# Two more expert outputs kept on the chip at the end of the second mixture of experts

## The chip, the core and the metric

The program runs on one core of a Trainium2 chip. The core has five engines with lists of instructions of their own: TensorE (PE in the profile, its weight loads as PEld), VectorE (DVE), ScalarE (ACT), GpSimd (POOL) and SyncE (SP, which here only issues transfers). Sixteen DMA engines move data between the chip's memory and the core's on-chip memory. The metric is the time of one execution on the device, in microseconds (us).

## The reference

Two transformer blocks run one after the other on 512 tokens of width 1024. Only the end of the second one is touched: a hierarchical mixture of experts. Every token picks one of four groups and two of the eight experts in it, so each of the 32 experts gets few tokens. What is computed there is

```python
combine = jnp.sum(one_hot(expert_idx, 32) * weights[..., None], axis=1)
y = zeros_like(hf)
for e in range(32):
    he = silu(hf @ w_gate[e]) * (hf @ w_up[e])
    y = y + combine[:, e:e+1] * (he @ w_down[e])
return x + y
```

with `w_gate[e]` and `w_up[e]` of 1024 x 256 and `w_down[e]` of 256 x 1024.

## The kernel before

Each expert of block 2 works on at most 64 slots (T = 64). `moe_experts_rows` (L1127) goes over the experts in 16 pairs. For each expert, `gather` brings its tokens into `xe` by products with a one-hot matrix, `gu` (L1172) multiplies by four gate/up weight tiles of 512 KB (line L1179) and applies SiLU, `htr` transposes the pair's result into `hT`, and `down` (L1198) multiplies by two down-weight tiles of 512 KB (L1208). `down` of a pair runs while `gu` of the next pair runs. The two halves of the 1024 output columns lie in the two halves of the 128 partitions, so an expert's output is one 128 x 512 tile.

What happens to that output differs by expert. `LAST` is the number of last experts whose outputs stay on the chip.

- Experts 0 to E - LAST - 1 (0 to 29 before): ACT or DVE scales the output into one of three buffers `yy` (L1218 for odd experts, L1220 for even ones), and POOL issues an indirect transfer that adds the rows to the accumulator `xa` in the chip's memory (L1221). This is called a scatter below. All scatters write `xa`, and each waits for the one before to land.
- Behind the scatter of expert E - LAST - 1, SP issues four loads of 512 KB that bring `xa` back into four buffers (`spare<-xa`, L1227). They are called base loads below. They wait for the last scatter.
- The last LAST experts (30 and 31 before): the output is split into a high part (ACT, L1213) and a low part (DVE, L1214) in a `spare` buffer.

`tokens` (L1135) makes one-hot matrices for these last experts on DVE (L1143), four tiles of 128 x 128 for each. At the end, for each of four token tiles and both column halves, `combined` multiplies the one-hot matrix with the high and the low parts (L1271), DVE adds the base tile (L1253), and the result is stored (L1255, L1261). Products for the two column halves use different 64 rows of PE and run side by side.

The weights are streamed by SP into 32 buffers of 512 KB (`more`, L801, issue on L823). A load waits until its buffer's reader is done and until the load four before it has landed. `spare` hands out weight buffers that are no longer needed. In `more`, two of them are set aside near the end of the stream for the one-hot matrices.

The order of instructions in each engine's list is fixed when the program is built: a scheduler with a simulated timeline merges the lists. SP takes its list strictly in order.

Of the kernel before, what the change touches and what calls it, by code (L numbers as in the profile page):

```python
# [12 lines left out]
F32R = mybir.dt.float32r  # L13
# [8 lines left out]
S = 512  # L22
# [32 lines left out]
class Kern:  # L55
# [745 lines left out]
    def more(self):  # L801


        n = len(self.places)
        while len(self.place) < len(self.seq):
            i = len(self.place)
            if i < n:
                pool, tag = self.places[i]
            else:
                while self.rows is None and self.place[self.prev][0] is None:  # L810
                    self.prev += 1
                if self.used <= self.prev:
                    return
                pool, tag = self.place[self.prev]
                self.prev += 1
                if pool is self.mw and len(self.free) < self.LAST and len(self.seq) - i <= 14:
                    self.free.append((pool, tag))
                    continue
            self.place.append((pool, tag))
            e, c = self.seq[i]  # L820
            raw = tag if pool is None else pool.tile([P, 1024], F32, tag=tag, name="raw", bufs=1)
            self.raws[e, c] = raw
            ld = self.nc.sync.dma_start(raw, self.wd[e, c - 4] if c > 3 else self.wgu[e, c])  # L823
            self.loads.append(ld.ins)
            under = self.FLIGHT if i >= n else self.FIRST
            if i >= under:
                self.tc.add_manual_dep(ld.ins, self.loads[i - under].name,
                                       mybir.DependencyInfo(mybir.DependencyClass.Sync, mybir.DependencyReason.DATA), reason="few under way")
# [298 lines left out]
    def moe_experts_rows(self, me):  # L1127
# [6 lines left out]

        def tokens():  # L1135

            st = [self.spare(F32R)[:, :S] for _ in range(LAST)]
            sh = me.tile([2 * T, LAST, NT], F32, name="sh")
            for t in range(NT):
                V.tensor_scalar(sh[:, :, t], self.sl[:, 0, E - LAST:], -128.0 * t, None, op0=OP.add)  # L1140
            for e in range(LAST):
                for t in range(NT):
                    V.tensor_scalar(st[e][:, t * P:(t + 1) * P], self.c("iota"), sh[:, e, t:t + 1], None, op0=OP.is_equal)  # L1143
            return st
# [88 lines left out]
        for p in range(E // 2 + 1):  # L1233
            e = 2 * p
            if e == E - 4:
                st = tokens()
            if e % 4 == 0:
                select(e + 4)
            for i in range(2):
                if e < E:  # L1240
                    gu(e + i)
                down(e + i - 2)
            if e < E:
                for q in range(2):
                    gather(e - e % 4 + 4, e % 4 + q)
                htr(p)
# [566 lines left out]
    def run(self, stage=99):  # L1813
# [59 lines left out]
            return  # L1873
        self.NG, self.NNAT, self.NPR, self.NATW = 6, 4, 7, 512
        nmw, nme = 19, 1
        self.LAST = 2
        self.NX, self.NY, self.FLIGHT = 0, 3, 4
        self.FIRST = 3
        xs, xl, short = [], [], ExitStack()
# [229 lines left out]
```

## Time and profile before

| | us |
|---|---|
| median of 3 runs | 1411.08 (1409.53 to 1414.77) |
| the profiled execution, its own time | 1408.74 |
| its span, first to last instruction | 1407.0 |
| PE busy | 1303.7 (93%) |
| DVE busy | 774.0 (55%) |
| ACT busy | 591.6 (42%) |
| POOL busy | 452.1 (32%) |

Times inside the execution are counted from the span's start. A timeline row gives start, length, engine, line, operation, output and inputs, the count, and in brackets how long the engine had been idle and what ended that.

### The profile page before, as it was taken

The numbers are of one execution on the slowest core, as the hardware profiler recorded it, in microseconds if no ns is written. First come the engines' busy times: TensorE is split into PE (matmuls) and PEld (weight loads), VectorE is DVE, ScalarE is ACT, GpSimd is POOL, SyncE is SP. The second block draws the span as 40 slices with busy tenths as digits, with TensorE's granted clock in tenths as the row PEclk, the third lists the DMA queues.
The fourth block names the chain that finished last, engine by engine and source line by source line (L and its number), as shares of the span: only waits on it lengthen the run. The fifth ranks groups of instructions, "written<-read, shape, count | busy, mean of one in ns | idle before, by whom it ended". The sixth has DMA issues, their size and how long they took to land.

```text
span 1407.0 us, 21509 instructions
## 1 busy us (share of the span) xinstructions
PE 1303.7 (93%) x8172; PEld 998.5 (71%) x8188; DVE 774.0 (55%) x1659; ACT 591.6 (42%) x1235; POOL 452.1 (32%) x368
## 2 busy tenths in 40 slices
PE   8898999869999798999999999999999799999983
PEld 8876777746665597987899999887789644545421
DVE  6899964858785856665455354224553723322222
ACT  5466442336664346654654354444223212221110
POOL 3354642422220336531143243123632302111211
PEclk9999999879999999999999999999999899999987
DMA  6122114889997211201121222226328589999994
GB/s 238 60 76 75 46 39 170 304 295 305 313 302 283 98 46 63 109 34 61 50 79 69 76 70 75 100 76 230 114 96 326 184 299 381 356 366 363 377 373 154
DMA packets 69124, 250.77 MB, mean 178 GB/s; under 512 B 12370, under 2 KB 12626, under 8 KB 62864
## 3 DMA queue, kind: packets, MB, share of 16 engines
q1 hardware_dynamic: 56304, 220.64, 43.2%
q0 software_dynamic: 11408, 25.24, 6.6%
q10 hardware_dynamic: 1296, 3.38, 0.6%
q8 instruction: 68, 1.11, 0.3%
q14 instruction: 48, 0.39, 0.1%
HBM read 230.29 MB, written 26.71 MB: 183 GB/s over the span
## 4 chain that ended last, share of the span: by engine, by line
PE 76%; DVE 13%; DMA 5%; ACT 2%; issue 2%; POOL 1%; SPq 0%; DVEq 0%; ACTq 0%; POOLq 0%
PE mm L181 13%; PE mm L183 13%; PE mm L182 13%; PE mm L1179 8%; PE tp L266 5%; PE pv L1164 5%; PE sc L1208 3%; DMA xa<-yy,idx 2%; PE pv L1759 2%; PE mm L1051 2%; DVE work L409 1%; DVE m L408 1%; PE sc L1733 1%; PE sc L1489 1%; DVE pr L707 1%
## 5 line engine op out<-in xcount | busy, mean ns | idle before, releaser
L154 POOL TENSOR_TENSOR wlo<-raw,whi 128x1024 fp32r<-128x1024 f32 (+4 forms) x62 | 149.6, 2416 | 252.5 <-ACT whi L153 231.9
L153 ACT ACTIVATE whi<-raw 128x1024 fp32r<-128x1024 f32 (+4 forms) x172 | 178.3, 1039 | 99.3 <-PE mm L183 42.4
L154 DVE TENSOR_TENSOR wlo<-raw,whi 128x1024 fp32r<-128x1024 f32 (+3 forms) x110 | 142.6, 1297 | 103.8 <-ACT whi L153 103.3
L1221 POOL DMA_INDIRECT xa<-yy,idx x30 | 46.4, 1548 | 220.3 <-DMA xa<-yy,idx 136.5
L183 PE MATMUL mm<-whi,hRl 128*128 128x256 f32 x384 | 108.8, 284 | 0.0
L181 PE MATMUL mm<-whi,hhi 128*128 128x256 f32 (+2 forms) x352 | 102.8, 292 | 4.8 <-ACT qraw L1428 1.8
L181 PE MATMUL mm<-whi,hRh 128*128 128x256 f32 x352 | 102.6, 292 | 0.0
L183 PE MATMUL mm<-whi,hlo 128*128 128x256 f32 (+2 forms) x352 | 101.5, 288 | 0.0
L182 PE MATMUL mm<-wlo,hhi 128*128 128x256 f32 (+2 forms) x352 | 101.0, 287 | 0.0
L1179 PE MATMUL mm<-raw,xe 128*64 128x512 f32 x396 | 100.6, 610 | 0.0
L182 PE MATMUL mm<-wlo,hRh 128*128 128x256 f32 x352 | 99.8, 283 | 0.0
L271 POOL TENSOR_TENSOR hss<-hss,mh 128x4 f32<-128x4 f32 (+1 forms) x64 | 60.1, 940 | 100.2 <-DVE hss L270 89.8
L181 PEld LDWEIGHTS mm<-whi,hhi 128*128 128x128 f32 x352 | 68.5, 195 | 10.5 <-issue 3.8
L183 PEld LDWEIGHTS mm<-whi,hRl 128*128 128x128 f32 x384 | 73.2, 191 | 0.0
L1186 DVE TENSOR_TENSOR gul<-gul,mm 64x512 f32<-64x512 f32 x32 | 21.9, 686 | 92.4 <-ACT gul L1185 92.4
L182 PEld LDWEIGHTS mm<-wlo,hhi 128*128 128x128 f32 x352 | 68.6, 195 | 1.6 <-issue 1.4
L183 PEld LDWEIGHTS mm<-whi,hlo 128*128 128x128 f32 x352 | 68.3, 194 | 1.4 <-issue 1.1
L1164 PEld LDWEIGHTS pv<-sel,xh 128*128 128x128 f32 x256 | 49.8, 194 | 27.2 <-issue 20.6
L1164 PE MATMUL pv<-sel,xh 128*128 128x256 f32 x256 | 67.1, 297 | 1.8 <-issue 1.8
L181 PEld LDWEIGHTS mm<-whi,hRh 128*128 128x128 f32 x352 | 67.2, 191 | 0.2
L182 PEld LDWEIGHTS mm<-wlo,hRh 128*128 128x128 f32 x352 | 67.2, 191 | 0.0
L1164 PE MATMUL pv<-sel,xl 128*128 128x256 f32 x256 | 65.6, 292 | 0.0
(537 smaller groups left out, 3634.4 us busy)
## 6 DMA issues: line engine op xcount, KB each, us to landing
raw<-in_wgu SPq DMA_DIRECT2D x163, 512.0 KB
raw<-in_wd SPq DMA_DIRECT2D x77, 512.0 KB
raw<-in_w2b SPq DMA_DIRECT2D x26, 1024.0 KB
rawp<-in_wgu SPq DMA_DIRECT2D x29, 512.0 KB
raw<-in_wo SPq DMA_DIRECT2D x12, 1024.0 KB
rawp<-in_wd SPq DMA_DIRECT2D x19, 512.0 KB
raw<-in_w1b SPq DMA_DIRECT2D x8, 1024.0 KB
spare<-xa SPq DMA_DIRECT2D x8, 512.0 KB
```

What stands on the lines that cost most here:

```text
L153: self.nc.scalar.activation(hi[:, :n], src, AF.Copy)
L154: eng.tensor_tensor(lo[:, :n], src, hi[:, :n].bitcast(F32), op=OP.subtract)
L181: nc.tensor.matmul(ps, lh, rh, start=start and i == 0, stop=False)
L182: nc.tensor.matmul(ps, lh, rl, start=False, stop=False)
L183: nc.tensor.matmul(ps, ll, rh, start=False, stop=stop and i == n - 1)
L266: self.nc.tensor.transpose(out, in_, self.c("ident")[:n, :n])
L271: return self.nc.gpsimd.tensor_tensor(out, out, self.mh[:, :n], op=OP.pow)
L1051: nc.tensor.matmul(pg[:T, :], x[2][:, j, :], wf[:, j * 512:(j + 1) * 512], start=False, stop=(j == 1))
L1164: nc.tensor.matmul(pg[:, j * 256:(j + 1) * 256], part[t][:, c], sels[e][:, t].rearrange("p e s -> p (e s)"), start=(i == 0), stop=(i == le ...
L1179: nc.tensor.matmul(pg[j * T:(j + 1) * T], x[:, 2 * c + j, e % 4], w[:, j * 512:(j + 1) * 512], start=(c == 0), stop=(c == 3))
L1208: nc.tensor.matmul(py[n * T:(n + 1) * T], hT[:, k, :], w[:, n * 512:(n + 1) * 512], start=(k == 0), stop=(k == 1))
L1221: nc.gpsimd.indirect_dma_start(out=xa2, out_offset=bass.IndirectOffsetOnAxis(ap=self.idx[:, 0, e:e + 1], axis=0), in_=y, in_offset=None, b ...
```

## The change

`LAST` of block 2 goes from 2 to 4. Experts 28 to 31 are kept on the chip, and 28 and 29 are scattered no more. The base loads belong to expert 27's `down` now. The one-hot matrices of two experts share one buffer of 128 x 1024, so four experts still need two buffers, and the count of buffers set aside in `more` stays two.

```diff
@@ more @@
-                if pool is self.mw and len(self.free) < self.LAST and len(self.seq) - i <= 14:
+                if pool is self.mw and len(self.free) < (self.LAST if self.rows is None else self.LAST // 2) and len(self.seq) - i <= 14:
@@ moe_experts_rows, tokens @@
-            st = [self.spare(F32R)[:, :S] for _ in range(LAST)]
+            st = [self.spare(F32R) for _ in range(LAST // 2)]
+            st = [st[i // 2][:, i % 2 * S:(i % 2 + 1) * S] for i in range(LAST)]
@@ run, block 2 @@
-        self.LAST = 2
+        self.LAST = 4
```

The diff does not show what the scheduler makes of it. On SP, at the end of the weight stream, the list before was as follows. `in_wd2` are down weights, `in_wgu2` gate/up weights, `xa_68` is the accumulator, and DMASW are the lanes of POOL's scatters.

```order
L823 DMA rawp_12009<-in_wd2 128x1024 [waits DMAHW4_49,PE_49]
L823 DMA rawp_12007<-in_wgu2 128x1024 [waits DMAHW5_49]
L823 DMA rawp_12010<-in_wd2 128x1024 [waits DMAHW6_49,PE_49]
L823 DMA rawp_12008<-in_wgu2 128x1024 [waits DMAHW7_49]
L823 DMA rawp_12013<-in_wd2 128x1024 [waits DMAHW0_49,PE_49]
L823 DMA rawp_12011<-in_wd2 128x1024 [waits DMAHW1_49,PE_49]
L823 DMA raw_13642<-in_wd2 128x1024 [waits DMAHW2_49,PE_49]
L823 DMA rawp_12012<-in_wd2 128x1024 [waits DMAHW3_49]
L1227 DMA spare_13808<-xa_68 128x1024 [waits DMASW2_49,DMASW1_49]
L1227 DMA spare_13810<-xa_68 128x1024
L1227 DMA spare_13812<-xa_68 128x1024 [waits DMASW3_49,PE_49]
L1227 DMA spare_13814<-xa_68 128x1024 [waits DMASW4_49,PE_49]
```

The same place on SP in the changed kernel:

```order
L823 DMA rawp_12009<-in_wd2 128x1024 [waits DMAHW4_49,PE_49]
L823 DMA rawp_12007<-in_wgu2 128x1024 [waits DMAHW5_49]
L1228 DMA spare_13764<-xa_68 128x1024 [waits DMASW1_49,DMASW0_49,PE_49]
L1228 DMA spare_13766<-xa_68 128x1024 [waits DMASW2_49,PE_49]
L1228 DMA spare_13768<-xa_68 128x1024 [waits DMASW3_49,PE_49]
L823 DMA rawp_12010<-in_wd2 128x1024 [waits DMAHW6_49]
L1228 DMA spare_13770<-xa_68 128x1024 [waits DMASW4_49,PE_49]
L823 DMA rawp_12008<-in_wgu2 128x1024 [waits DMAHW7_49]
L823 DMA rawp_12013<-in_wd2 128x1024 [waits DMAHW0_49]
L823 DMA rawp_12011<-in_wd2 128x1024 [waits DMAHW1_49]
L823 DMA raw_13642<-in_wd2 128x1024 [waits DMAHW5_49,DMAHW2_49]
L823 DMA rawp_12012<-in_wd2 128x1024 [waits DMAHW7_49,DMAHW3_49]
```

The four base loads have moved from behind the last weight load to a place six weight loads earlier (three base loads, one weight load, the fourth base load, then five weight loads). Everything ahead of them in SP's list is as before. `rawp_12010` holds down weights of expert 29, `rawp_12008` the last gate/up weights of expert 31, and the other four the down weights of 30 and 31.

On PE, around the second half of expert 29's `down` (`sc` from `rawp_12010`) and the last part of expert 31's `gu` (`mm` from `rawp_12008`), the list before:

```order
L1179 MATMUL mm_13785<-rawp_12007,xe_13487 64x512 [waits DMAHW1_49]
L1179 MATMUL mm_13785<-rawp_12007,xe_13487 64x512
L1208 MATMUL sc_13798<-rawp_12010,hT_13759 64x512 [waits DMAHW2_49]
L1208 MATMUL sc_13798<-rawp_12010,hT_13759 64x512
L1179 MATMUL mm_13785<-rawp_12008,xe_13487 64x512 [waits DMAHW3_49]
L1179 MATMUL mm_13785<-rawp_12008,xe_13487 64x512
L266 MATMUL tp_13816<-cf_58,gul_13770 128x128 [waits DVE_49]
L266 MATMUL tp_13816<-cf_58,gul_13770 128x128
L1208 MATMUL sc_13821<-rawp_12011,hT_13819 64x512 [waits DMAHW5_49,DVE_49]
L1208 MATMUL sc_13821<-rawp_12011,hT_13819 64x512
```

The same place in the changed kernel, with the first one-hot products, which read expert 28's output `spare_13796`:

```order
L1180 MATMUL mm_13799<-rawp_12007,xe_13487 64x512 [waits DMAHW1_49]
L1180 MATMUL mm_13799<-rawp_12007,xe_13487 64x512
L1272 MATMUL pv_13851<-spare_13796,spare_13694 128x512 [waits Activation_49]
L1272 MATMUL mm_13862<-spare_13796,spare_13694 128x512 [waits DVE_49]
L1272 MATMUL pv_13893<-spare_13796,spare_13694 128x512
L1272 MATMUL pv_13851<-spare_13796,spare_13694 128x512 [waits DVE_49]
L1272 MATMUL mm_13862<-spare_13796,spare_13694 128x512
L1272 MATMUL pv_13893<-spare_13796,spare_13694 128x512
L1209 MATMUL sc_13812<-rawp_12010,hT_13775 64x512 [waits DMAHW5_49]
L1209 MATMUL sc_13812<-rawp_12010,hT_13775 64x512
L1272 MATMUL pv_13851<-spare_13817,spare_13694 128x512 [waits Activation_49]
L1272 MATMUL mm_13862<-spare_13817,spare_13694 128x512
```

There are 64 one-hot products instead of 32. Part of those for experts 28 and 29 stand between the last weight products; 44 of the 64 stand after the last product that reads a weight, where all 32 stood before.

## Rows read from the trace of the kernel before

**Rows 1.** The page: shares of the chain that ended last; DMA busy tenths in 40 slices.

```profile
PE 76%; DVE 13%; DMA 5%; ACT 2%; issue 2%; POOL 1%; SPq 0%; DVEq 0%; ACTq 0%; POOLq 0%
...
DMA  6122114889997211201121222226328589999994
```

**Rows 2.** The chain of waits from 1352 us on: start, us, what.

```profile
1360.91 7.49 DMA xa<-yy,idx
...
1369.14 5.85 DMA xa<-yy,idx
...
1375.73 3.69 DMA xa<-yy,idx
...
1380.30 3.86 DMA xa<-yy,idx
...
1384.90 3.75 DMA xa<-yy,idx
...
1390.34 7.94 DMA spare<-xa
```

**Rows 3.** Waits of SP's queue, 1330 to 1400 us: total us, times, longest.

```profile
SPq L1227 <- DMA xa<-yy,idx: 18.8, 1, 18.8
```

**Rows 4.** Timeline of SP's issues, 1355 to 1400 us.

```profile
1360.77 0.33 SPq L823 DMA_DIRECT2D rawp<-in_wgu  x1
...
1363.33 0.33 SPq L823 DMA_DIRECT2D rawp<-in_wgu  x1
...
1369.57 0.33 SPq L823 DMA_DIRECT2D rawp<-in_wd  x1
1388.71 2.01 SPq L1227 DMA_DIRECT2D spare<-xa  x4
```

**Rows 5.** Windows: us, busy by engine, PEclk, DMA share, GB/s.

```profile
1364.00:1368.00 4.00, 4.00 (x10) 1.13 (x12) 0.42 (x1) 0.00 (x0) 0.00 (x0) 0.50 1.00 335
...
1378.00:1382.00 4.00, 3.40 (x10) 1.21 (x12) 0.45 (x2) 0.00 (x0) 1.54 (x1) 0.57 0.10 16
...
1397.00:1402.00 5.00, 0.00 (x0) 0.00 (x0) 2.57 (x4) 0.00 (x0) 0.00 (x0) 0.50 0.92 365
1402.00:1407.00 5.00, 0.00 (x0) 0.00 (x0) 0.00 (x0) 0.00 (x0) 0.00 (x0) 0.50 0.07 27
```

**Rows 6.** Timeline of DVE: one-hot matrices, low parts, final adds.

```profile
1343.51 0.89 DVE L1143 TENSOR_SCALAR spare<-cf,sh 128x128 fp32r<-128x128 f32 x4 [0.97 <-PE mm L1179]
1345.84 0.69 DVE L1186 TENSOR_TENSOR gul<-gul,mm 64x512 f32<-64x512 f32 x1 [1.45 <-ACT gul L1185]
...
1383.98 1.61 DVE L1214 SCALAR_TENSOR_TENSOR spare<-sc,gs,spare 128x512 fp32r<-128x512 f32 x2 [5.00 <-ACT spare L1213]
1392.05 0.69 DVE L1253 TENSOR_TENSOR spare<-spare,sc 128x512 f32<-128x512 f32 x1 [6.46 <-DMA spare<-xa]
...
1397.05 0.69 DVE L1253 TENSOR_TENSOR spare<-spare,sc 128x512 f32<-128x512 f32 x1 [1.79 <-issue]
...
1398.97 0.68 DVE L1253 TENSOR_TENSOR spare<-spare,tp 128x512 f32<-128x512 f32 x1
```

**Rows 7.** Timeline of PE, 1371 to 1389 us.

```profile
1374.65 1.02 PE L1179 MATMUL mm<-rawp,xe 128*64 128x512 f32 x4
...
1379.03 3.31 PE L1208 MATMUL sc<-rawp,hT 128*64 128x512 f32 x8 [0.52 <-DVE hT L1196]
1382.18 1.02 PE L1208 MATMUL sc<-raw,hT 128*64 128x512 f32 x4
1383.04 1.02 PE L1208 MATMUL sc<-rawp,hT 128*64 128x512 f32 x4
1384.88 0.48 PE L1271 MATMUL sc<-spare 64*128 64x512 f32 x1 [0.81 <-ACT spare L1213]
...
1388.50 0.39 PE L1271 MATMUL mm<-spare 64*128 64x512 f32 x1
```

**Rows 8.** Timeline of ACT: the last scaled output for a scatter.

```profile
1375.10 0.69 ACT L1218 ACTIVATE yy<-sc,gs 128x512 f32<-128x512 f32 x1 [4.48 <-DMA xa<-yy,idx]
```

## The prediction

> **What bounds the kernel now.** I read the page's chain shares and DMA slices first. PE carries 76% of the chain over the whole span, but the DMA slices are at 8 to 9 tenths through the end [rows 1], so the end needs a look of its own. The chain of waits shows it: from 1360.91 us on, no PE work stands in it at all. There is one scatter after another, each issued when the one before has landed, then a base load, then DVE's adds [rows 2]. The five rows shown are the scatters of experts 25 to 29. SP's queue says the same from its side: the first base load stood 18.8 us at the head of SP's list, waiting for the scatters [rows 3]. The last weight load had been issued at 1369.57, the base loads at 1388.71 [rows 4]. PE was done with weights at 1384.06 and with the one-hot products at 1388.89 [rows 7], and DVE still waited until 1392.05 for base data [rows 6]. So the last 9 us before 1388.7 belong to two scatters and nothing else, and after 1388.7 the end is base loads, adds and stores.
>
> **What is removed.** Scatters 28 and 29 leave the chain. Expert 27's scatter landed at 1375.73 + 3.69 = 1379.42, expert 29's at 1384.90 + 3.75 = 1388.65: 9.2 us. ACT's wait for a free `yy` buffer before expert 29 (4.48 us) goes too [rows 8], but it gains nothing: PE finished the products that ACT takes next at 1375.67 [rows 7], when that ACT row was running.
>
> **What is moved, and why it takes the gain back.** SP's list now has three base loads, a weight load, the fourth base load and five weight loads where it had six weight loads and then four base loads. SP takes its list in order, and the 18.8 us show that it stands still while the first base load waits. So six weight loads of experts 29 to 31, which were issued from 1362.1 to 1369.57, now wait for scatter 27. The weights were early before; now they are the last thing to come.
>
> Step one, when does scatter 27 land? The stream stops after the load issued at 1360.77. Four loads are then under way; at 1.28 us each (two steps from 1360.77 to 1363.33 took 2.56 [rows 4]) they drain by 1365.9. Scatter 25 is issued at 1360.91 with 5.0 us of loads beside it. Scatter 26 had 4.8 us of loads beside it (the last load, issued at 1369.57, was one of four and drained by about 1374) and took 5.85, where 25 had taken 7.49 under the full stream; scatters alone take 3.7 to 3.9 [rows 2]. The DMA share was 1.00 in the one stretch and 0.10 in the other [rows 5]. I give scatter 25 5.9 us, scatters 26 and 27 3.75 each, and 0.73 us between a landing and the next issue (1360.91 + 7.49 to 1369.14): 1360.91 + 5.9 + 0.73 + 3.75 + 0.73 + 3.75 = 1375.8, and the first base load goes at 1375.9. The ends are 1373.7 (all three at 3.75) and 1379.5 (nothing gets faster). The Trainium skill, "DMA: Bandwidth & Descriptors", section "Queues, rings and completion order", says that each DMA engine takes turns between the queues that have work, packet by packet; by it a scatter is slowed only while loads stand beside it, which gives the 1375.9, and the kernel before agrees with its 3.69 against 7.49. A scatter bound by its own fixed steps would give 1379.5.
>
> Step two, the ten loads. The first base load of before was used 1392.05 - 1388.71 = 3.34 us after its issue. Nine more at 1.28 put the last down weights at 1375.9 + 3.34 + 11.5 = 1390.8. (Before, four base loads took until 1398.28, but stores ran beside them.) The last gate/up load is the sixth and lands at 1385.6. From the end of those products to the first `down` product took 1379.03 - 1375.67 = 3.36 us before [rows 7]. With 0.9 us for its own products that is 1389.9, so it hides under the last load, by less than 1 us.
>
> Step three, from the last weights to the last add. Three pairs of `down` products of 0.43 us (the row of four took 0.86 to the next [rows 7]) end at 1392.1. High and low parts took from 1384.06 to 1385.59 before [rows 6], so the last low part is ready at 1393.6. Of the 64 one-hot products 44 stand behind the last weight product. The 32 of before took 4.0 us, 0.125 each, with the two column halves side by side [rows 7]. The first token tile's sum now has six products of one half in a row and twelve others ahead of it. I take 2.2 us from the last low part to the first add (1.0 would be PE's own last products; 4.4 the same at half the clock): 1395.8. Four adds took 1397.05 to 1399.65, 2.6 us [rows 6]; eight take 5.2. Last add: 1401.0, against 1399.65 before.
>
> Step four, the tail. From the last add to the span's end was 1407.0 - 1399.65 = 7.35 us. Now all 2 MB of stores leave within 4 us instead of 6; at the 365 GB/s of the stretch 1397 to 1402 [rows 5] they need 5.7 us and end some 0.6 us later than the last store alone would. Span: 1401.0 + 7.35 + 0.6 = 1409.0, that is 2.0 us more than 1407.0.
>
> **Edits at no cost.** Sixteen one-hot tiles instead of eight: eight more DVE instructions of 0.22 us (four in 0.89), in two groups. In the second group 0.9 us more fits in the 1.45 us that DVE was idle before its next row [rows 6]; the first stands in a similar gap. If the cover were gone it would be 1.8 us. Two more high/low pairs replace two scalings on ACT and DVE and stand before the late weights. The number of buffers set aside is the same, so the weight stream up to the base loads is unchanged.
>
> **Rivals.** One, the path simply gets 9.2 us shorter: if the end still hung on base loads alone, they would start at 1379.5 instead of 1388.7 and the time would be 1411.1 - 9.2 = 1402. The chain and the 18.8 us speak for it; the six weight loads behind the wait speak against it. It needs their 3 MB to arrive with nothing waiting on them, and PE's list waits on each.
>
> Two, on the other side: PE falls to the lower clock and stays there. In 1364 to 1368 the granted clock was 0.50 (1.2 GHz), after a pause of PE, and in 1378 to 1382 it was 0.57, after another [rows 5]; eight products took 3.15 us there and four 0.86 just after [rows 7], about twice as long each. The new gap, while SP waits (about 1374 to 1383), is longer than those, and after it PE works in short pieces between single loads. If the clock were still at half from the last weights to the last sum, the `down` products would cost 1.3 us more and the 44 one-hot products, at about 0.125, some 5.5 us more, nearly all ahead of the last add: 1409.0 + 6.5 = 1415.5 of span, 1419.6 as a median. The point that decides is whether the clock is back at 1.0 by about 1391. Before, PE got work again at 1379.03 and was at full speed at 1382.18 [rows 7]. The Trainium skill, "TensorE: Matmul & The Clock Gate", section "HAM oscillation — how this bites in real kernels", describes this case: waits for data between groups of products put PE back to half the clock each time. The trace agrees with it in both gaps; whether it lasts is not shown.
>
> Three, scatters 25 to 27 are no faster without the stream: the base loads go at 1379.5, and the time is 3.6 us over the forecast, 1416.7.
>
> **How the numbers follow.** The profiled execution took 1408.74 us, 1.74 more than its span and 2.3 below the median; the change of +2.0 is put on the median: 1413.1. The likeliest case alone spans 1409 to 1417. Chances: this forecast 0.72, rival one 0.06, rival two 0.14, rival three 0.08. Measurement tells about 0.5%, 7 us, from no change: below 1404.0 is faster, above 1418.1 slower. Rival one is the faster chance, 0.06. Slower is rival two with a little of the others' upper ends, 0.16. The rest is 0.78. The range 1407 to 1420 leaves out rival one and what lies past rival two.
>
> **What would show it.** In the changed kernel's profile: SP's longest wait is again the base load on the scatters, but ends near 1376; DMA is nearly idle from about 1366 until then; expert 31's gate/up weights land near 1386 and the last down weights near 1391, and PE waits for them; the last scatter takes about 3.7 us; the last add ends near 1401. The prediction is wrong if the base loads do not hold the weights up (last weights before 1385), if the clock stays at 0.50 past 1391, or if the ten loads take clearly more than 15 us.

## The result and the profile after

The changed kernel took 1419.1 us (median of 8 runs, 1416.4 to 1423.6), the kernel before 1408.6 us on the same chip (8 runs, 1405.1 to 1414.8). The ratio is 1.0075, 95% interval 1.0055 to 1.0094: slower by 10.6 us, and by more than the 0.5% that the prediction counted as no change. The profiled execution took 1418.33 us, with a span of 1416.6 against 1407.0 before.

The page first: the shares of the chain are those of [rows 1] almost to the digit, so the page alone tells nothing. The chain of waits (start, us, what), which answers to [rows 2], shows what came in:

```profile
1358.66 6.89 DMA xa<-yy,idx
...
1366.29 3.73 DMA xa<-yy,idx
...
1370.76 3.68 DMA xa<-yy,idx
...
1375.82 6.83 DMA rawp<-in_wd
1382.70 2.00 PE sc L1209 x4
...
1394.69 5.34 PE sc L1209 x16
```

The two last scatters of [rows 2] are gone, and the last one left, expert 27's, ends at 1374.44. But where a base load and adds followed before, PE now stands in the chain from 1382.70 on. This execution issued expert 25's scatter at 1358.66, 2.25 us earlier than the profiled one of before. SP's waits and its timeline, beside [rows 3, 4]:

```profile
SPq L1228 <- DMA xa<-yy,idx: 14.7, 1, 14.7
```

```profile
1359.41 0.33 SPq L823 DMA_DIRECT2D rawp<-in_wgu  x1
1374.49 1.28 SPq L1228 DMA_DIRECT2D spare<-xa  x3
1375.82 0.42 SPq L823 DMA_DIRECT2D rawp<-in_wd  x1
1376.34 0.40 SPq L1228 DMA_DIRECT2D spare<-xa  x1
1376.79 0.44 SPq L823 DMA_DIRECT2D rawp<-in_wgu  x1
1377.28 0.92 SPq L823 DMA_DIRECT2D rawp<-in_wd  x2
1382.72 0.33 SPq L823 DMA_DIRECT2D raw<-in_wd  x1
1385.27 0.33 SPq L823 DMA_DIRECT2D rawp<-in_wd  x1
```

No weight is asked for between 1359.41 and 1375.82. Six weight loads, which left by 1369.57 before, leave behind the first base loads. Of these, expert 31's last gate/up weights, issued at 1376.79, took 8.4 us to land, at 1385.2 (the last number of this line of the DMA issues):

```profile
rawp<-in_wgu SPq DMA_DIRECT2D x1, 512.0 KB, 8.4
```

The last load took 5.0 us and landed at 1390.3. PE's timeline and windows (us, busy by engine, PEclk, DMA share, GB/s), beside [rows 7, 5]:

```profile
1382.70 1.98 PE L1209 MATMUL sc<-rawp,hT 128*64 128x512 f32 x4 [10.81 <-DMA rawp<-in_wd]
...
1386.61 1.98 PE L1180 MATMUL mm<-rawp,xe 128*64 128x512 f32 x4
...
1394.62 4.55 PE L1209 MATMUL sc<-rawp,hT 128*64 128x512 f32 x12
1399.00 1.02 PE L1209 MATMUL sc<-raw,hT 128*64 128x512 f32 x4
```

```profile
1366.00:1368.00 2.00, 2.00 (x12) 0.58 (x10) 1.10 (x2) 0.68 (x2) 1.56 (x1) 1.00 0.00 0
...
1390.00:1394.00 4.00, 4.00 (x9) 2.59 (x10) 0.85 (x2) 0.39 (x1) 0.00 (x0) 0.50 0.00 0
1394.00:1398.00 4.00, 4.00 (x10) 1.00 (x10) 0.00 (x0) 0.00 (x0) 0.00 (x0) 0.50 0.00 0
1398.00:1402.00 4.00, 4.00 (x25) 2.34 (x23) 1.50 (x2) 1.38 (x2) 0.00 (x0) 0.98 0.00 0
```

PE waited 10.81 us. The granted clock fell during this wait (0.54 in 1374 to 1378) and was 0.50 (1.2 GHz) until 1398. In 1390 to 1398 next to no data was under way (DMA share 0.00) and PE was busy without a break: its own half speed was then the limit. Four records of `down` products took 1.98 us at 1382.70 and 1.02 at 1399.00. DVE, beside [rows 6]:

```profile
1343.37 1.66 DVE L1144 TENSOR_SCALAR spare<-cf,sh 128x128 fp32r<-128x128 f32 x8 [0.97 <-PE mm L1180]
1345.70 0.69 DVE L1187 TENSOR_TENSOR gul<-gul,mm 64x512 f32<-64x512 f32 x1 [0.68 <-ACT gul L1186]
...
1400.80 0.75 DVE L1215 SCALAR_TENSOR_TENSOR spare<-sc,gs,spare 128x512 fp32r<-128x512 f32 x1 [0.98 <-ACT spare L1214]
1403.84 0.69 DVE L1254 TENSOR_TENSOR spare<-spare,sc 128x512 f32<-128x512 f32 x1 [2.29 <-PE tp L1272]
...
1408.04 0.68 DVE L1254 TENSOR_TENSOR spare<-spare,tp 128x512 f32<-128x512 f32 x1
```

The first add starts at 1403.84 where 1395.8 was forecast, and the last ends at 1408.72 where 1401.0 was forecast.

### The profile page after: what moved, and what is told of

The parts are those of the page before. It is cut to its first block, busy times and chain, and to the rows that moved or that the text cites. A ratio compares the mean times of both kernels' runs of the same rounds, so it can differ in the third digit from the quotient of the medians.

```text
span 1416.6 us, 21589 instructions
## 1 busy us (share of the span) xinstructions
PE 1313.3 (93%) x8220; PEld 1001.5 (71%) x8220; DVE 776.1 (55%) x1668; ACT 591.9 (42%) x1236; POOL 449.3 (32%) x366
## 3 DMA queue, kind: packets, MB, share of 16 engines
q8 instruction: 68, 1.11, 0.3%
## 4 chain that ended last, share of the span: by engine, by line
PE 76%; DVE 13%; DMA 5%; issue 3%; ACT 2%; POOL 1%; SPq 0%; POOLq 0%; ACTq 0%; DVEq 0%
PE mm L181 13%; PE mm L183 13%; PE mm L182 13%; PE mm L1180 7%; PE tp L266 5%; PE pv L1165 5%; PE sc L1209 4%; DMA xa<-yy,idx 3%; PE pv L1760 2%; PE mm L1051 2%; DVE work L409 2%; DVE m L408 1%; PE sc L1734 1%; PE sc L1490 1%; DVE pr L707 1%
```

## The experiments

My theory after the result: the six weight loads held up behind the base loads cost the whole difference, partly by coming late and partly by what the gap does to PE's clock. The rivals: something else in the change is dear (shared rows, more one-hot products), or the two scatters were never worth 9 us. Ratios are to the kernel before, run on the same chip (medians 1407.8 to 1409.7 us).

Each edit makes the scheduler merge the lists anew, so the order of PE's last products differs somewhat between these kernels. From the first of the last eight `down` products on, that costs nothing: from its start to the first add it was 7.44 to 7.50 us in all seven traces that have the clock at 1.00 there, in two different orders (9.22 in the changed kernel, at half the clock for half of it). Ahead of expert 31's last gate/up product it does cost, as is told where it matters.

**Base loads on SP, behind the six weight loads.** On SP this undoes the move alone. In PE's list, the three one-hot products that stand between expert 29's second `down` half and expert 31's last gate/up product go behind the latter.

```
+ with ExitStack() as behind:
+     for ld in self.loads[-6:]:
+         behind.enter_context(self.tc.issue_after(ld))
      self.order = [nc.sync.dma_start(self.base[t], ...)]
```

> The changed kernel with one edit: the four base loads stay on SP but are kept behind the last six weight loads in its list. Theory: same as with the base loads on POOL, span 1400 to 1403, ratio 0.995 to 0.997, because only the place in SP's list matters and not which queue carries the loads. If the other queue matters (two queues share the DMA engines differently), this one differs from the POOL kernel by more than 2 us. Rival A (one-hot products cost what the scatters gave): ratio 1.000 or above.

Measured: 1401.1 us (6 runs), ratio 0.9942 (0.9920 to 0.9964). Its SP timeline, PE timeline, windows and first add:

```profile
1382.82 1.75 SPq L1231 DMA_DIRECT2D spare<-xa  x4
```

```profile
1376.06 1.08 PE L1209 MATMUL sc<-rawp,hT 128*64 128x512 f32 x4
1376.97 1.03 PE L1180 MATMUL mm<-rawp,xe 128*64 128x512 f32 x4
```

```profile
1382.00:1386.00 4.00, 4.00 (x19) 1.54 (x20) 0.39 (x1) 0.69 (x1) 0.00 (x0) 1.00 0.55 193
1386.00:1390.00 4.00, 4.00 (x27) 2.96 (x28) 1.57 (x3) 0.69 (x1) 0.00 (x0) 1.00 0.89 323
```

```profile
1389.54 0.69 DVE L1257 TENSOR_TENSOR spare<-spare,sc 128x512 f32<-128x512 f32 x1 [1.05 <-PE sc L1275]
```

The base loads leave only when scatter 27 has landed, as in the changed kernel, but nothing stands behind them: the last weight load went at 1373.07. From 1374 to 1390 PE is busy for 15.9 of 16 us at a clock of 1.00, and the first add waits for PE, not for a base load. So two scatters fewer are worth 8.2 us (0.0058 of 1407.8), and holding up six weight loads turns that into a loss of 10.6: it costs 18.8 us, give or take 4. At most 1.4 us of it can be the three one-hot products that stand elsewhere: in the changed kernel the gate/up product began that much after its weights had landed (1386.61 against 1385.2). This version beats both kernels.

**Base loads issued by POOL.** Another way to clear SP's list.

```
- self.order = [nc.sync.dma_start(self.base[t], ...)]
+ self.order = [nc.gpsimd.dma_start(self.base[t], ...)]
```

> The changed kernel with one edit: the four base loads are issued by POOL, behind the scatters in its own list, and not by SP. SP's list then holds weight loads alone. Theory (the loss is SP standing still with six weight loads behind the base loads, and the clock that falls in the pause): the weights land by about 1375 us again, the base loads start near 1379.5 and land by about 1388, the first add starts near 1388, and the span is 1400 to 1403, 4 to 7 us under the kernel before (ratio 0.995 to 0.997). Rival A (the 32 extra one-hot products and splits cost what two scatters gave): 1407 or more, ratio 1.000 or above. Rival B (the scatters and base loads themselves got slower): span near 1416, ratio near 1.0075.

Measured: 1408.1 us, ratio 0.9994 (0.9976 to 1.0011). The weights are on time, the last of them issued at 1373.49, and yet 7 us are missing against the run above. Its PE timeline, windows and first add:

```profile
1375.66 1.08 PE L1209 MATMUL sc<-rawp,hT 128*64 128x512 f32 x4
...
1378.97 1.08 PE L1180 MATMUL mm<-rawp,xe 128*64 128x512 f32 x4
1381.47 1.45 PE L1272 MATMUL mm<-spare 64*128 64x512 f32 x4 [1.41 <-DVE gul L1187]
...
1385.46 3.68 PE L1209 MATMUL sc<-rawp,hT 128*64 128x512 f32 x8
```

```profile
1382.00:1386.00 4.00, 4.00 (x11) 1.92 (x11) 0.74 (x2) 0.00 (x0) 1.95 (x4) 0.53 0.74 255
1386.00:1390.00 4.00, 4.00 (x12) 1.14 (x8) 0.00 (x0) 0.00 (x0) 0.00 (x0) 0.62 0.72 271
```

```profile
1395.46 0.69 DVE L1254 TENSOR_TENSOR spare<-spare,sc 128x512 f32<-128x512 f32 x1 [1.79 <-PE sc L1272]
```

From expert 29's second `down` half to the first add it is 19.8 us here and 13.5 in the run above: 6.3 of the 7 us lie there. PE's list differs: expert 31's last gate/up product stands behind six one-hot products more, for which PE waited 0.79 us. It starts 3.3 us after that `down` half instead of 0.9, which is 2.4 us. The other 3.9 come behind it: PE was idle for 1.41 us, and the clock then fell to half for some 7 us. By the two windows the half clock took at most 3.4 us of PE's time (an estimate: 4 us times 0.47 and 4 us times 0.38). Three theories: the order of PE's list, the half clock, or POOL as the issuer.

**POOL as the issuer in the kernel before**, the same edit there:

> The kernel before with its four base loads issued by POOL instead of SP. There the base loads stand behind all weight loads anyway, so nothing can be held up by them. If POOL's queue costs about the same as SP's: ratio 1.000 within 0.003, last add within 1.5 us of the 1399.65 of before. If issuing base loads from POOL is itself dear (the rival for why the run with base loads on POOL came out some 6 us above the one that keeps them on SP behind the weights): ratio 1.003 to 1.006.

Measured: ratio 0.9997 (0.9981 to 1.0013). Issuing from POOL costs nothing there that the interval would show.

**POOL and eight products more**, result unused, right behind expert 31's last gate/up product:

```
+ if e == 31:
+     with self.tc.issue_after(mm.ins):
+         warm = bank("pv")
+         for i in range(8):
+             nc.tensor.matmul(warm, st[0][:, :P], self.last[0][1][0], ...)
```

> The changed kernel with base loads issued by POOL, and with 8 extra one-hot products, result unused, right behind expert 31's last gate/up product, where TensorE stood idle for 0.8 and 1.4 us in the run without them and fell to half clock from 1382 to 1390. If that half clock is what separates base loads on POOL (1408.1) from base loads on SP behind the weights (1401.1): clock at 1.0 throughout 1378 to 1392, ratio 0.993 to 0.997. If POOL's queue or the later base loads are what costs: clock at 1.0 and ratio 0.998 to 1.001. If the clock falls again, nothing is told apart: ratio about 1.000.

Measured: 1405.3 us, ratio 0.9965 (0.9947 to 0.9983). By the medians, eight products of useless work made it faster by 0.3%, though the two intervals overlap a little. The windows, expert 29's second `down` half and the first add:

```profile
1374.00:1378.00 4.00, 4.00 (x14) 2.71 (x15) 1.11 (x2) 0.77 (x2) 1.03 (x3) 0.60 0.40 115
1378.00:1382.00 4.00, 4.00 (x20) 2.11 (x19) 0.42 (x1) 0.00 (x0) 1.49 (x3) 1.00 0.93 284
```

```profile
1369.55 1.08 PE L1214 MATMUL sc<-rawp,hT 128*64 128x512 f32 x4
```

```profile
1388.24 0.69 DVE L1259 TENSOR_TENSOR spare<-spare,sc 128x512 f32<-128x512 f32 x1 [2.27 <-PE sc L1277]
```

The clock dipped earlier, while the eight products ran (3.68 us), and was back before the last `down` products. From expert 29's second `down` half to the first add it is 18.7 us, 1.1 less than without the eight products. The ratios differ by 0.0029, 4 us, with an interval of some 0.6 to 7.6, which holds the 1.1. So the half clock is a part of the 7 us, but how it shares them with the order of PE's list is not shown.

**Only the shared rows**: the changed kernel with two experts kept instead of four.

```
- self.LAST = 4
+ self.LAST = 2
```

> The changed kernel with two last experts kept on the chip instead of four (so all thirty scatters of before); what is left of the change is that one-hot rows share room. SP's list is that of before. If that part is free, as the prediction has it: ratio 0.998 to 1.002. If it carries part of the loss: 1.003 or more.

Measured: ratio 1.0002 (0.9987 to 1.0017). That part is free, as the prediction had it. The 32 one-hot products more are not in this kernel; they are in the first experiment's, which beats the kernel before.

**Base loads that wait for no scatter**, still ahead of the six weight loads. They read another buffer of the same size, so the scattered sums are left out of the output.

```
- ... self.xa[t * P:(t + 1) * P, :]
+ ... self.xr[t * P:(t + 1) * P, :]   # issued behind the loads of two earlier chunks
```

> The changed kernel with the base loads in their early place on SP (now all four ahead of the six weight loads), but reading another array of the same size that was written long before, so that they wait for no scatter. The scattered sums are left out of the output. Theory (the wait costs, not the 2 MB in front of the weights): base loads go out near 1361 us, the last weights land near 1380 instead of 1390, PE has no long pause, and the span is 1400 to 1405, ratio 0.995 to 0.999. Rival (four more transfers ahead of the weights cost by themselves as much as the wait): the last weights land near 1385 or later and the span is over 1408, ratio 1.001 or above.

Measured: 1405.4 us, ratio 0.9987 (0.9969 to 1.0006), span 1403.1. Without the wait the loss is gone: it is the waiting base load at the head of the list that costs (all weight loads were issued by 1377.04 here). It is not as fast as with base loads behind the weights; its clock was 0.68 in 1378 to 1382.

**Filling the gap.** To price the half clock apart from the late weights, 48 useless one-hot products were put in front of the product that waits (expert 29's second `down` half).

```
+ if e == 29 and k == 1:
+     warm = bank("pv")
+     for i in range(48):
+         nc.tensor.matmul(warm, st[0][:, :P], self.last[0][1][0], ...)
```

> The changed kernel with 48 extra one-hot products on PE (128 rows, 512 columns, result not used) placed in its list just ahead of the product that waits for the held-up weights, so that PE is busy during the pause. SP's list is the changed kernel's, word for word. Theory (of the changed kernel's 9.6 us loss about 7 are the half clock, which lasted to about 1398 us, and 2 the late weights): the clock stays at 1.0 through the pause, the last weights land near 1390 as in the changed kernel, the last add ends near 1401 instead of 1408.7, and the span is 1408 to 1411, ratio 1.001 to 1.003. If the clock falls again in the short waits after 1383, 1411 to 1414. Rival (the clock is only a sign of waiting, the weights are the whole loss): 1416 to 1418, ratio 1.0065 to 1.008.

Measured: 1414.0 us, ratio 1.0042 (1.0025 to 1.0059). The clock stayed at 1.00 until 1386 and then fell to 0.62 in 1386 to 1390, beside two waits for weights of 1.50 and 1.08 us. So a second attempt had 64 products, in front of expert 31's last gate/up product:

```
+ if e == 31 and c == 3:
+     behind.enter_context(self.tc.issue_after(mm.ins))
+     warm = bank("pv")
+     for i in range(64):
+         wm = nc.tensor.matmul(warm, st[0][:, :P], self.last[0][1][0], ...)
+     behind.enter_context(self.tc.issue_after(wm.ins))
```

> The changed kernel with 64 extra one-hot products, result unused, in front of expert 31's last gate/up product, where TensorE otherwise waits from 1371 to 1386 us: about 14.9 us of work at 0.233 us each, ending as the gate/up weights land. Transfers and SP's list are those of the changed kernel. Theory (late weights cost about 2 us, the half clock after the gap the other 7 to 8): the granted clock stays 1.0 until the last sum, first add 1395.5 to 1398, span 1408.5 to 1411.5, ratio 1.000 to 1.003. Rival one (the late weights themselves cost most of it): clock at 1.0 and span still 1414 or more, ratio 1.004 to 1.008. Rival two (the clock falls all the same in the short waits that are left): 1411 to 1414, and the windows show 0.6 or less somewhere in 1386 to 1394.

Measured: 1417.0 us, ratio 1.0046 (1.0030 to 1.0062). PE, one window, SP and the first add; this execution's scatters were some 7 us behind the changed kernel's already at 1300 us, so only differences count:

```profile
1377.60 14.80 PE L1184 MATMUL pv<-spare 128*128 128x512 f32 x64
1393.51 1.08 PE L1187 MATMUL mm<-rawp,xe 128*64 128x512 f32 x4 [1.11 <-DMA rawp<-in_wgu]
...
1399.17 2.79 PE L1216 MATMUL sc<-rawp,hT 128*64 128x512 f32 x12
```

```profile
1390.00:1394.00 4.00, 2.89 (x15) 1.87 (x15) 0.00 (x0) 0.00 (x0) 0.00 (x0) 1.00 1.03 420
```

```profile
1381.67 1.28 SPq L1235 DMA_DIRECT2D spare<-xa  x3
```

```profile
1406.62 0.69 DVE L1261 TENSOR_TENSOR spare<-spare,sc 128x512 f32<-128x512 f32 x1 [2.27 <-PE sc L1279]
```

The clock was 1.00 in every window from 1374 to 1406, and rival one's ratio came: 1.0046, not the 1.000 to 1.003 of my theory. From the first base load to the first add it is 24.95 us here, 29.35 in the changed kernel and 19.9 in the forecast. So the half clock is worth 4.4 us there, and 4.1 by the ratios (0.0029 of 1409, with an interval of some 0.6 to 7.6). The other 6.5 us of the loss are in the late weights themselves, and that is after the 8.2 us which the scatters are worth: of the 18.8 us some 4 are the half clock and the rest, 14 to 15, the late weights.

**Three of four base loads behind the weights.** The first still waits at the head.

```
- for ld in self.loads[-6:]:
+ for ld in self.loads[-6:] if t else ():
```

(against the first experiment's edit.)

> The changed kernel with the first base load still at the head of SP's list, so that all six weight loads still wait for scatter 27, but the other three base loads behind the six weight loads. TensorE's list and scatters are little changed. It takes away 3.8 us (three loads of 1.28 us) from the time to the last weights, and leaves the wait itself and the gap. Theory (loads land one after another in the order of the list, so what stands ahead of the weights is paid in full): expert 31's gate/up weights land 5.5 to 7 us after the first base load is issued instead of 10.7, the last weights about 11 instead of 15.8, and the first add comes 4 to 5 us earlier; ratio 1.001 to 1.004 (the half clock remains). Rival (the three base loads shared the queues and cost little, and the price is the wait and the clock): ratio 1.005 to 1.008.

Measured: 1412.0 us, ratio 1.0021 (1.0000 to 1.0042). The landing of the gate/up weights, SP, PE, one window and the first add:

```profile
rawp<-in_wgu SPq DMA_DIRECT2D x1, 512.0 KB, 5.7
```

```profile
1376.61 0.33 SPq L1231 DMA_DIRECT2D spare<-xa  x1
```

```profile
1381.13 1.98 PE L1209 MATMUL sc<-rawp,hT 128*64 128x512 f32 x4 [6.17 <-DMA rawp<-in_wd]
1383.22 1.97 PE L1180 MATMUL mm<-rawp,xe 128*64 128x512 f32 x4
```

```profile
1386.00:1390.00 4.00, 3.80 (x16) 1.87 (x16) 1.40 (x3) 0.41 (x1) 0.00 (x0) 1.00 1.01 408
```

```profile
1396.72 0.69 DVE L1257 TENSOR_TENSOR spare<-spare,sc 128x512 f32<-128x512 f32 x1 [1.05 <-PE sc L1275]
```

The gate/up weights, issued at 1377.46, land 6.6 us after the first base load instead of 10.7. These 4.1 us answer to three loads of 1.28 (3.8): the loads are served in the list's order, and what stands ahead of the weights is paid for. The gate/up product starts when they land, 6.6 us after the base load instead of 12.1; the 1.4 us on top are PE's, which in the changed kernel still had three one-hot products at half the clock ahead of it and waited 0.79 us for them. The first add comes 20.1 us after that base load instead of 29.35, 9.2 us earlier and not 4 to 5. The 3.7 us that are left lie between the gate/up product and the first add (13.5 us instead of 17.2), where the clock was back from 1386 on. By the ratios the gain is 7.6 us, give or take 4.

**The same with 36 useless products in the gap.**

```
- for i in range(64):
+ for i in range(36):
```

> The same with 36 extra one-hot products, result unused, in front of expert 31's last gate/up product: 8.4 us of work where TensorE would wait from 1371 to about 1380 us. Theory: clock at 1.0 to the end; what is left is the wait for scatter 27 alone; ratio 0.997 to 1.000, about 4 us (0.3%) under the run without the products. If the clock falls all the same, or the half clock has no price once the gap is shorter: within 0.15% of that run. If the time is still 1.003 or more with the clock at 1.0, the price lies in the chain of products behind the weights, not in the order of the loads.

Measured: 1411.7 us, ratio 1.0009 (0.9994 to 1.0024), not told apart from the run before it. PE still waited 2.69 us for the gate/up weights, and the clock was 0.65 in 1386 to 1390. It did not isolate the wait for scatter 27.

## Why the prediction was wrong, and where it was right

The forecast was a change of +2.0 us; it was +10.6. The range held the time only because its upper end had been set by rival two, and rival two, at 0.14, happened: the clock was not back by 1391 but only at 1398, which the prediction had named as a sign of being wrong. The outcome "slower" had been given 0.16.

- **Step one held.** Scatters 25 to 27 took 6.89, 3.73 and 3.68 us (forecast 5.9, 3.75, 3.75), and the first base load left at 1374.49 (1375.9). The moment is partly luck: from scatter 25's issue to the base load it was 15.8 us where 15.0 was forecast, and the execution was 2.25 us early at scatter 25. The DMA share of 0.00 in 1366 to 1368 stands beside the 3.73. That is what the Trainium skill's turns between queues ("DMA: Bandwidth & Descriptors", section "Queues, rings and completion order") would give; rival three, scatters as slow as before, is out.
- **Step two held for the loads**: the last weights landed at 1390.3 (1390.8), 15.8 us after the first base load where 14.9 was forecast. Expert 31's gate/up weights landed 10.7 us after it, where 9.7 was forecast; in the runs with 48 and 64 products, where PE waited for these weights, their products began 11.3 and 11.8 us after it. I have no cause for these 1 to 2 us.
- **The end of step two and step three failed**, in two ways. Step two ended with "With 0.9 us for its own products that is 1389.9, so it hides under the last load, by less than 1 us". It did not hide. From the start of the gate/up products to the first of the last `down` products it was 8.0 us (1386.61 to 1394.62) where 4.3 was forecast; with the base loads behind the weights, at full clock, it was 5.1. The chain from the gate/up weights over activation, transposes and `down` products is the path, and the first of the last `down` products began at 1394.62, waiting for no load. Step three let three pairs of products at 0.43 us, 1.3 us, follow the last load. What follows is eight products (sixteen records) in one piece, behind eleven one-hot products and two transposes: 3.65 us at full clock (1393.19 to 1396.84 in the run with 48 products), and 5.34 here. And the clock, which step three took as full from 1391 on, was at half until 1398.
- **The ledger from the first base load to the first add**: forecast 19.9, measured 29.35. To the start of the gate/up products 12.1 instead of 9.7 (+2.4: 1.0 until the weights landed, 1.4 until PE came to them). From there to the first add 10.2 forecast, 12.6 at full clock with the base loads behind the weights, 13.1 in the run with 64 products at full clock (+2.4 to +2.9; in the latter expert 29's products come later), 17.2 in the changed kernel (+4.1 to +4.7, the clock). The span grew by 9.6 us, 7.6 more than forecast: the 9.45 of this ledger and 0.8 from step one, less the 2.25 us by which this execution was early at scatter 25 and 0.4 us in the adds and the tail.
- **Rival two was right by its sign and its deciding point; its 1419.6 is partly luck.** Over the kernel before, it put 6.5 us on the clock and 2.0 on the weights; the runs put about 4 on the clock and 6.5 on the weights. The rule of the Trainium skill that it was named beside ("TensorE: Matmul & The Clock Gate", section "HAM oscillation — how this bites in real kernels") agrees with this trace: after PE's wait for data the clock was at half, and with the wait filled it was 1.00 throughout. That it would last to 1398 with PE busy from 1390 on was what the trace of before could not show, and I gave it too little: PE waited 10.81 us, where the waits beside the two falls in the kernel before were 4.89 and 2.40, and PE's work after it came in short pieces. PE's timeline before:

```profile
1363.27 0.69 PE L266 MATMUL tp<-cf,gul 128*128 128x128 f32 x2 [4.89 <-DVE gul L1188]
...
1378.08 0.44 PE L266 MATMUL tp<-cf,gul 128*128 128x128 f32 x2 [2.40 <-DVE gul L1188]
```

- **Rival one was wrong for this kernel.** Its 1402 is what the version with base loads behind the weights took (1401.1), but not by its path: there the base loads left at 1382.82 and not at 1379.5, and the first add waited for PE. That the numbers meet is luck.
- **Step four and the free edits held.** From the last add to the span's end 7.88 us (forecast 7.95); from the last low part to the first add 2.29 (2.2), the clock being back by then. The eight adds took 4.9 us (5.2). Eight one-hot tiles in one group took 1.66 us and left DVE 0.68 us idle before its next row, where 0.55 was forecast; the run with two experts kept shows the shared rows free.

## What to carry to other kernels

When a change lets a load wait earlier in an in-order list, look at what stands behind it there, and move it behind those first: here one edit of the order is the difference between a loss of 10.6 us and a gain of 8.2. Follow the products that late data release to the end before calling them hidden, with the whole row of products that the list puts together. And where a new gap leaves PE idle, price what follows at half the clock too, and give that case real weight: in these runs the clock stood at 0.50, 0.58 and 0.65 behind waits of 10.81, 6.17 and 2.69 us.

## What was not expected of the hardware

In the changed kernel the clock stayed at 0.50 from 1378 to 1398, eight of these microseconds with PE busy without a break; in the run with three base loads moved it was back within about 4 us of PE's return (1381.13; 0.58 in 1382 to 1386, 1.00 after). Waits of 0.79 and 1.41 us stood ahead of a fall to 0.53 in the run with base loads on POOL, while in the run with 64 products a wait of 1.11 us left the clock at 1.00. In that POOL run, eight useless products of 3.68 us did not make the end longer: from expert 29's second `down` half to the first add it was 1.1 us less.
